# Changing the order of a convolution's inverse transforms, and the queue of attention's loads, in a two-layer diffusion trunk

## The chip, the cores and the metric

The kernel runs on one core of a Trainium2 chip. The metric is the device time of one execution in microseconds; several runs are made and their median is taken. A separate execution is profiled; its trace shows every instruction with its engine, start, duration and the tiles that it writes and reads. Five engines work beside each other: TensorE (PE, with its weight loads as PEld), VectorE (DVE), ScalarE (ACT), GpSimd (POOL) and SyncE (SP). Each takes its instructions in order. DMA transfers are issued from the instruction stream of an engine, here from SP or from POOL.

## The reference

The input is a sequence of 1024 latent tokens and 256 context tokens of width 1024. Layer 0 normalises and projects them once; half of the channels go through neighbourhood attention (8 heads of 64; each query sees a window of 8 x 16 grid places and all context keys), the other half through a bidirectional gated delta rule. Layer 1 is a Hyena layer: two long convolutions by FFT with gates between. Cut to what the change touches:

```python
def one_row(r):                     # neighbourhood attention, for each of 16 grid rows
    s_win = jnp.einsum('bqhd,brqkhd->bhqrk', qr, kw) + bias
    s_ctx = jnp.einsum('bqhd,bkhd->bhqk', qr, kc)
    p = jax.nn.softmax(jnp.concatenate([s_win.reshape(b, h, GRID_W, nwin), s_ctx], axis=-1), axis=-1)
    return p_win @ vw + p_ctx @ vc

def long_conv(u, h_fwd, h_bwd, skip):
    y_f = irfft(rfft(u, n) * rfft(h_fwd, n), n)[:length]
    y_b = irfft(rfft(u[::-1], n) * rfft(h_bwd, n), n)[:length][::-1]
    return y_f + y_b + u * skip

z = x1 * long_conv(v, filt[:, 0, 0], filt[:, 0, 1], skip[0])    # first convolution
y = x2 * long_conv(z, filt[:, 1, 0], filt[:, 1, 1], skip[1])    # second convolution
return s + gate * ((y * silu(g)) @ w_out)
```

All data are float32. Large products are made from float32r parts: a value is split into a rounded high part and the rest, the low part, and three of the four partial products are added up (`mm3`, `gemm_steps`).

## The kernel before

Everything runs on tiles of 128 partitions. A scheduler at build time gives each engine's instructions a fixed order, by priorities and a simulated time line. Two things bind it. Matrix products and transposes that go through `mm` (L116) and `tr` (L121) are pinned while `self.pinned` is set, so PE works in the order in which the program is written. And `keep_in_program_order` pins an instruction behind the one that was written just before it for the same engine; other instructions may move ahead.

**Filler.** PE's order is woven by hand. `self.fill(n)` takes n products from a generator of independent matrix products and puts them between two steps whose data need time. In attention the filler is `dn_out` (the delta heads' part of layer 0's output projection, accumulator `do`, added to `dx` in L1128 and stored by SP in L1129). In layer 1 it is `hy_stream`, the input projection.

**Attention (`natten`).** The heads are worked on in 4 pairs p; a pair has 8 column blocks j and 2 heads u, so there are 64 units in a row. A unit's scores are four products (`na_scores`): the query tile nq against the high and the low part of the keys, nkh and nkl, once for the context and once for the window. DVE adds the bias nbias and reduces (L1059), ACT takes the exponential (L1060). Two units later PE transposes the result (`na_transpose`, pt) and DVE and ACT copy it (pts, L1073); two units after that the values are multiplied (`na_values`, pv), and DVE finishes with L1094 and L1095.

`na_unit` prepares a pair and head: the bias is loaded from SP (L1016), and nq, nkh and nkl by six transfers from POOL (L1021). Each of the six fills 64 partitions, from 64 rows of the scratch arrays nq_d and nk_d that the projection stage has written: for v = 0 partitions 0 to 63, for v = 1 partitions 64 to 127. The query tile has its high part above its low part; each key tile has the same rows twice. The tiles are of type float32r, and the source is read as float32r by a bitcast. Sizes are 256 KB for nq and 320 KB for nkh and nkl. For the first pair all transfers are issued before the loop. For pair p + 1 they begin at unit 4 of pair p, two at a time, all pinned; two sets of buffers take turns.

SP issues nearly all other transfers: the raw tiles dyr (L1103) and dx (L1106) of `dn_out`, the output weights ewo_raw (L1372), the values bnv and the gate ny. `split` then makes the two parts of a raw tile: the high part on ACT (L102, for example dyh), the low part on POOL or DVE (L105). ewo_raw is first multiplied by a gate on POOL (L1384).

**Layer 1.** For each of 8 channel blocks there are two convolutions, objects of the class `Conv`: `first` on v, `second` on z. Each goes through the steps fold, transpose, dft, bins, product, idft and unfold, and the loop in `layer1` weaves the two together:

```python
second.product(); first.dft(); first.bins(); self.fill(FILL_D[2])
second.idft(); ...; y = second.unfold(); ...
first.product(); self.fill(FILL_D[3]); first.idft()
```

(FILL_D[2] is 20, FILL_D[3] is 64, and 56 products come before the next transpose.) `bins` writes the spectrum U on DVE (L1741 to L1744; the last two read the accumulator bo). `product` multiplies it with the filter's spectrum in U itself (L1753 to L1762, L1758 and L1759 being the last for the part that is used directly). Then it makes W, the high and low part of some rows of U: hWh on ACT (L1766) and hWl on DVE (L1767), each in a small piece and a large one. Last it makes Z on DVE (L1769 and L1770). `idft` then multiplies Z, one part of U, and W with the inverse matrices. It has four accumulators of 512 columns, p1, q1, pq2 and pq3 (the trace calls them p, q and pq), which come from a pool of four buffers, the same that `dft` uses for be, bo and br of the other convolution. `unfold` needs pq3 for its first step, pq2 for its second, and p1 and q1 for its third.

Of the kernel before, what the change touches and what calls it, by code (L numbers as in the profile page):

```python
# [10 lines left out]
F32 = mybir.dt.float32  # L11
F32R = mybir.dt.float32r
# [8 lines left out]
P = 128  # L21
# [40 lines left out]
class Kernel:  # L62
# [944 lines left out]
    def na_unit(self, p, u, nb):  # L1007

        nc = self.nc
        nm = f"{p}{u}"  # L1010
        rows = slice(64 * u, 64 * u + 64)
        q = nb.tile([P, L], F32R, name="nq" + nm, tag="nq")
        k = [nb.tile([P, LA], F32R, name=f"nk{n}" + nm, tag="nk" + n) for n in "hl"]
        bias = nb.tile([P, 1152], F32, name="nbias" + nm, tag="nbias")
        keep = self.tc.keep_in_program_order
        loads = [lambda: (keep if p else lambda ins: ins)(nc.sync.dma_start(bias, self.ap["na_bias"][2 * p + u]))]  # L1016
        for v in range(2):
            half = slice(64 * v, 64 * v + 64)
            for dst, src in ((q, self.nq_d[p][v]), (k[0], self.nk_d[p][0]), (k[1], self.nk_d[p][1])):
                loads.append(lambda dst=dst[half], src=src[rows, :]:  # L1020
                             keep(nc.gpsimd.dma_start(dst, src.bitcast(F32R))))  # L1021
        return (q, *k, bias), loads

    def na_pair(self, p):
# [631 lines left out]
    def idft(self, ps, Y, mat):  # L1656
        for k, y in enumerate(Y):
            self.mm(ps, y, mat[:, k, :], start=k == 0, stop=k == len(Y) - 1)

    def unfold(self, y, p, z, m):  # L1660

        nc = self.nc
        h = m // 2
        pat = {2: "p m -> p m", 3: "p (m b) -> p m b", 4: "p (m b two) -> p m b two"}[len(p.shape)]
        kw = {2: {}, 3: {"b": 2}, 4: {"b": 2, "two": 2}}[len(p.shape)]
        a, b, c = (t.rearrange(pat, **kw) for t in (y[:, 0:h], y[:, m:h:-1], z[:, 0:h]))
        nc.vector.tensor_tensor(a, p, c, ALU.add)
        nc.vector.tensor_tensor(b, c, p, ALU.subtract)
        nc.vector.tensor_copy(y[:, h:h + 1], z[:, h:h + 1])


class Conv:
# [99 lines left out]
    def idft(self):  # L1772
        k, mats, W, Z = self.k, self.mats, self.W, self.Z
        p1, q1, pq2, pq3 = self.ps = [self.psf.tile([P, 512], F32, name=n + self.nm, tag="f")
                                      for n in ("p1", "q1", "pq2", "pq3")]
        for b in range(2):
            sl = slice(b * P, b * P + P)
            k.idft(pq2[:, sl], [Z[:, 0, b, :]], mats[f"ia{b}"])
            k.idft(pq2[:, 256 + b * P:384 + b * P], [Z[:, 1, b, :]], mats[f"ib{b}"])
            k.idft(p1[:, sl], [Z[:, 0, 2 + b, :]], mats[f"ia{b}"])  # L1780
            k.idft(q1[:, 256 + b * P:384 + b * P], [Z[:, 1, 2 + b, :]], mats[f"ib{b}"])
        k.idft(pq3[:, 0:128], [self.U[:, 0, 6, :]], mats["ia0"])
        k.idft(pq3[:, 128:256], [self.U[:, 1, 6, :]], mats["ib1"])
        for ps, terms in ((pq3[:, 256:512], ((0, 2, "icc", 0), (1, 2, "iss", 0))),
                          (p1[:, 256:512], ((0, 0, "ico", 0), (0, 1, "ico", 1))),
                          (q1[:, 0:256], ((1, 0, "iso", 0), (1, 1, "iso", 1)))):
            terms = [t + ab for ab in PARTS for t in terms]
            for i, (s, j, name, n, a, b) in enumerate(terms):
                k.mm(ps, W[b][:, s, j, :], mats[name + "r"][a][:, n, :], start=i == 0, stop=i == len(terms) - 1)

    def unfold(self):
        k, nc = self.k, self.k.nc
# [164 lines left out]
```

## Time and profile before

| | us |
|---|---|
| median of 3 runs | 1907.99 |
| lowest, highest | 1900.15, 1911.63 |
| profiled execution | 1902.58 |
| its span, first to last instruction | 1900.8 |

The granted clock of PE is 0.96 of full speed over the span. In 40 slices of 47.5 us each, a digit is the busy share in tenths:

```profile
PE   6799988899998997999988899889999999999898
...
DVE  5899988756677834555566565759999989999876
...
DMA  8545455222424557454589863543433432443344
```

Attention is in slices 20 to 24 (of 0 to 39), where the DMA engines are busiest after the start. Layer 1's loop runs from about slice 27 to slice 38; there DVE is nearly as busy as PE.

In answers of the trace, a row names engine, line, operation and `out<-in` tiles, and in brackets how long the engine stood idle before it and what ended that. Times are from the start of the span. The instruction named as having ended a wait is the one that finished last by the profile; another that finished just before can be the true one.

### The profile page before, as it was taken

The page shows a single profiled execution, that of the slowest core. Times are in us where ns is not written, and L with a number is a line of the kernel's source. Part 1 is how long each engine was busy: PE and PEld are TensorE (multiplying, and loading weights), DVE is VectorE, ACT ScalarE, POOL GpSimd, SP SyncE. Part 2 cuts the span into 40 slices and gives each one's busy share as a digit, 9 for nine tenths or more (in the row PEclk, how much of TensorE's full clock was granted, in tenths as well). Part 3 has the DMA queues.
Part 4 walks back from the last instruction along what each step waited for, and adds up shares of the span by engine and source line. Part 5 has one row for each costly group of instructions (what it writes and reads, how often), then busy time and mean ns, then how long its engine had stood idle before and what let it go on. Part 6 is the DMA issues. An engine that isn't in the chain of part 4 may idle for free.

```text
span 1900.8 us, 30378 instructions
## 1 busy us (share of the span) xinstructions
PE 1734.8 (91%) x11124; PEld 1408.9 (74%) x11124; DVE 1417.5 (75%) x2847; ACT 842.6 (44%) x1830; POOL 582.4 (31%) x860
## 2 busy tenths in 40 slices
PE   6799988899998997999988899889999999999898
PEld 2366755688886775878877787778788788888686
DVE  5899988756677834555566565759999989999876
ACT  4557574444535432333344444544343434434321
POOL 0665554310193865721035401330000000000410
PEclk9889997999997998999999999999999999999999
DMA  8545455222424557454589863543433432443344
GB/s 287 167 117 158 136 187 170 107 73 103 149 94 116 163 173 229 145 131 155 158 230 230 227 192 85 185 113 93 121 108 83 105 104 72 113 128 106 108 131 139
DMA packets 162912, 270.53 MB, mean 142 GB/s; under 512 B 76953, under 2 KB 98985, under 8 KB 160714
## 3 DMA queue, kind: packets, MB, share of 16 engines
q1 hardware_dynamic: 152538, 230.83, 38.4%
q0 software_dynamic: 10224, 37.75, 10.2%
q8 instruction: 88, 1.44, 0.3%
q14 instruction: 62, 0.51, 0.1%
HBM read 192.50 MB, written 76.03 MB: 141 GB/s over the span
## 4 chain that ended last, share of the span: by engine, by line
PE 59%; DVE 21%; DMA 8%; POOL 4%; ACT 4%; issue 3%; SPq 1%; DVEq 0%; ACTq 0%; POOLq 0%
PE hx L116 6%; PE fo L116 4%; PE hg L116 3%; PE pa L116 3%; PE hu L116 2%; PE nk L116 2%; PE nv L116 2%; PE nq L116 2%; PE pq L116 2%; DVE ff L1169 2%; PE z L116 2%; PE dn L112 2%; PE dn L110 2%; PE dn L111 2%; PE pv L116 2%
## 5 line engine op out<-in xcount | busy, mean ns | idle before, releaser
L763 POOL TENSOR_TENSOR sub<-Lb,Xb 80x31 f32<-80x31 f32 (+15 forms) x124 | 87.2, 703 | 67.4 <-DMA Lb<-lsc_d 39.7
L116 PE MATMUL hx<-h1h,w1x_lo 128*128 128x512 f32 x256 | 101.0, 395 | 0.3 <-DMA w1x_lo<-in_w 0.3
L116 PE MATMUL hx<-h1l,w1x_hi 128*128 128x512 f32 x256 | 101.1, 395 | 0.0
L116 PE MATMUL hx<-h1h,w1x_hi 128*128 128x512 f32 x256 | 100.9, 394 | 0.0
L112 PE MATMUL dn<-hh,wdn_lo 128*128 128x512 f32 (+1 forms) x256 | 95.0, 372 | 0.9 <-DVE wdn_lo L105 0.9
L110 PE MATMUL dn<-hh,wdn_hi 128*128 128x512 f32 (+1 forms) x256 | 94.7, 370 | 0.0
L111 PE MATMUL dn<-hl,wdn_hi 128*128 128x512 f32 (+1 forms) x256 | 94.6, 370 | 0.0
L660 DVE SCALAR_TENSOR_TENSOR dacc<-dpad,convw,dacc 128x1024 f32<-128x1024 f32 (+1 forms) x80 | 75.9, 977 | 21.1 <-ACT dacc L658 20.2
L765 POOL TENSOR_TENSOR Xb<-Xb,sub 80x31 f32<-80x31 f32 (+15 forms) x124 | 82.9, 668 | 9.1
L1060 ACT ACTIVATE pr<-pr,st 128x640 f32<-128x640 f32 (+1 forms) x64 | 51.3, 802 | 54.1 <-DVE st L1059 54.0
L121 PE MATMUL pt<-ident,pr 128*128 128x128 f32 x304 | 46.4, 278 | 11.0 <-ACT pts L1073 6.7
L112 PEld LDWEIGHTS dn<-hh,wdn_lo 128*128 128x128 f32 x256 | 48.7, 190 | 9.8 <-DVE wdn_lo L105 1.3
L1180 ACT COPY fx<-fx_ps 128x512 f32<-128x512 f32 (+1 forms) x96 | 43.4, 484 | 27.9 <-PE fx_ps L121 24.6
L116 PEld LDWEIGHTS hx<-h1h,w1x_lo 128*128 128x128 f32 x256 | 48.1, 188 | 9.5 <-DMA w1x_lo<-in_w 0.7
L121 PE MATMUL fx_ps<-ident,ff 128*128 128x128 f32 x288 | 49.9, 299 | 5.7 <-ACT fx L1180 3.6
L1289 PE MATMUL fh<-fhh,w3s 128*128 128x512 f32 x64 | 38.2, 599 | 18.6 <-DVE fh L1291 18.6
L116 PEld LDWEIGHTS hx<-h1h,w1x_hi 128*128 128x128 f32 x256 | 48.1, 188 | 9.0
L116 PEld LDWEIGHTS hx<-h1l,w1x_hi 128*128 128x128 f32 x256 | 48.2, 188 | 8.9
L111 PEld LDWEIGHTS dn<-hl,wdn_hi 128*128 128x128 f32 x256 | 48.8, 191 | 8.0 <-issue 0.5
L110 PEld LDWEIGHTS dn<-hh,wdn_hi 128*128 128x128 f32 x256 | 48.8, 191 | 7.4
L121 PEld LDWEIGHTS pt<-ident,pr 128*128 128x128 f32 x304 | 36.3, 141 | 22.4 <-ACT pts L1073 9.3
L1313 POOL TENSOR_TENSOR fp<-fh,fh 128x1024 f32<-128x1024 f32 x16 | 39.4, 2461 | 42.4 <-ACT fh L1299 42.4
(576 smaller groups left out, 5920.1 us busy)
## 6 DMA issues: line engine op xcount, KB each, us to landing
hG<-g_d SPq DMA_DIRECT2D x16, 1088.0 KB
g_d<-G SPq DMA_DIRECT2D x16, 1024.0 KB
em_w<-in_em_w SPq DMA_DIRECT2D x24, 512.0 KB
om_w<-in_om_w SPq DMA_DIRECT2D x24, 512.0 KB
wz_raw<-in_w0z SPq DMA_DIRECT2D x16, 512.0 KB
w1x_raw<-in_w SPq DMA_DIRECT2D x16, 512.0 KB
w1x_lo<-in_w POOLq DMA_DIRECT2D x16, 512.0 KB, 7.6
wdn_raw<-in_w0dn SPq DMA_DIRECT2D x12, 512.0 KB
```

Source lines behind the costliest of these rows:

```text
L110: nc.tensor.matmul(ps, wh, xh, start=start, stop=False)
L111: nc.tensor.matmul(ps, wh, xl, start=False, stop=False)
L112: nc.tensor.matmul(ps, wl, xh, start=False, stop=stop)
L116: ins = self.nc.tensor.matmul(*args, **kw)
L121: ins = self.nc.tensor.transpose(out, x, self.ident)
L660: nc.vector.scalar_tensor_tensor(acc[:, t0:t0 + n], pad[:, o + j:o + j + n], cw[:, blk, j:j + 1], acc[:, t0:t0 + n], ALU.mult, ALU.add)
L763: nc.gpsimd.tensor_tensor(tv, Lb[:, j + 1:, j:j + 1].broadcast_to([80, m, c]), Xb[:, j:j + 1, 0:c].broadcast_to([80, m, c]), ALU.mult)
L765: nc.gpsimd.tensor_tensor(Xb[:, j + 1:, 0:c], Xb[:, j + 1:, 0:c], tv, ALU.subtract)
L1060: nc.scalar.activation(pr[:, :n], pr[:, :n], AF.Exp, bias=st[:, 0:1], scale=-1.0, accum_out=st[:, 1:2])
L1180: nc.scalar.copy(out[:, j0:j0 + m, :].rearrange("p a b -> p (a b)"), ps[:, :m * P])
L1289: nc.tensor.matmul(ps, ws[:, od, :], hh[:, sl], start=True, stop=False)
L1313: nc.gpsimd.tensor_tensor(pp[:, :L], hf[:, :L], hb[:, :L], ALU.add)
```

## The change

Two places are edited.

`na_unit`: the transfers of nq, nkh and nkl are issued from SP, except those with p = 0 and v = 0, which stay on POOL. On SP they are written as plain float32 words: the destination is read as float32 by a bitcast, the source is left as it is. They stay pinned by `keep_in_program_order`, now on SP's queue. 42 of the 48 transfers move.

`Conv.idft`: the loop over Z's eight products is moved from the beginning to the end. U's two products and the three groups of W products come first. The products themselves, their accumulators and `unfold` are the same.

```diff
@@ na_unit
             for dst, src in ((q, self.nq_d[p][v]), (k[0], self.nk_d[p][0]), (k[1], self.nk_d[p][1])):
-                loads.append(lambda dst=dst[half], src=src[rows, :]:
-                             keep(nc.gpsimd.dma_start(dst, src.bitcast(F32R))))
+
+                eng = nc.sync if p or v else nc.gpsimd
+                loads.append(lambda dst=dst[half], src=src[rows, :], eng=eng:
+                             keep(eng.dma_start(*((dst, src.bitcast(F32R)) if eng is nc.gpsimd else (dst.bitcast(F32), src)))))
@@ Conv.idft
-        for b in range(2):
-            sl = slice(b * P, b * P + P)
-            k.idft(pq2[:, sl], [Z[:, 0, b, :]], mats[f"ia{b}"])
-            k.idft(pq2[:, 256 + b * P:384 + b * P], [Z[:, 1, b, :]], mats[f"ib{b}"])
-            k.idft(p1[:, sl], [Z[:, 0, 2 + b, :]], mats[f"ia{b}"])
-            k.idft(q1[:, 256 + b * P:384 + b * P], [Z[:, 1, 2 + b, :]], mats[f"ib{b}"])
+
         k.idft(pq3[:, 0:128], [self.U[:, 0, 6, :]], mats["ia0"])
         k.idft(pq3[:, 128:256], [self.U[:, 1, 6, :]], mats["ib1"])
         for ps, terms in ((pq3[:, 256:512], ((0, 2, "icc", 0), (1, 2, "iss", 0))),
                           (p1[:, 256:512], ((0, 0, "ico", 0), (0, 1, "ico", 1))),
                           (q1[:, 0:256], ((1, 0, "iso", 0), (1, 1, "iso", 1)))):
             terms = [t + ab for ab in PARTS for t in terms]
             for i, (s, j, name, n, a, b) in enumerate(terms):
                 k.mm(ps, W[b][:, s, j, :], mats[name + "r"][a][:, n, :], start=i == 0, stop=i == len(terms) - 1)
+        for b in range(2):
+            sl = slice(b * P, b * P + P)
+            k.idft(pq2[:, sl], [Z[:, 0, b, :]], mats[f"ia{b}"])
+            ...
```

More of the change, by code (lines that the diff above doesn't have):

```diff
@@ L1789, in idft @@
                 k.mm(ps, W[b][:, s, j, :], mats[name + "r"][a][:, n, :], start=i == 0, stop=i == len(terms) - 1)
+        for b in range(2):
+            sl = slice(b * P, b * P + P)
+            k.idft(pq2[:, sl], [Z[:, 0, b, :]], mats[f"ia{b}"])
+            k.idft(pq2[:, 256 + b * P:384 + b * P], [Z[:, 1, b, :]], mats[f"ib{b}"])
+            k.idft(p1[:, sl], [Z[:, 0, 2 + b, :]], mats[f"ia{b}"])
+            k.idft(q1[:, 256 + b * P:384 + b * P], [Z[:, 1, 2 + b, :]], mats[f"ib{b}"])
     def unfold(self):
```

## The prediction

> **What bounds the kernel now.** I read the page first: engine shares, then the chain of waits that ended last.
>
> ```profile
> span 1900.8 us, 30378 instructions
> ## 1 busy us (share of the span) xinstructions
> PE 1734.8 (91%) x11124; PEld 1408.9 (74%) x11124; DVE 1417.5 (75%) x2847; ACT 842.6 (44%) x1830; POOL 582.4 (31%) x860
> ...
> PE 59%; DVE 21%; DMA 8%; POOL 4%; ACT 4%; issue 3%; SPq 1%; DVEq 0%; ACTq 0%; POOLq 0%
> ```
>
> TensorE (PE) is busy 91% of the span, so an edit pays only where it shortens one of PE's waits or the half-clock stretch that follows a long one. VectorE (DVE) comes second. The change touches two stages, so next comes the table by stage: attention (950 to 1180 us), and two turns of the second layer's loop over channel blocks, an early one and a late one. Columns: length, then the busy time of PE, PEld, DVE, ACT and POOL, PE's clock, the DMA share and GB/s.
>
> ```profile
> 950.00:1180.00 230.00, 207.01 (x1696) 174.04 (x1695) 148.59 (x408) 107.46 (x285) 69.92 (x83) 0.98 0.76 195
> ...
> 1356.00:1423.00 67.00, 63.16 (x360) 54.72 (x360) 60.41 (x96) 25.22 (x40) 4.12 (x23) 0.97 0.39 101
> ...
> 1690.00:1757.00 67.00, 66.29 (x385) 57.62 (x384) 62.13 (x97) 28.47 (x45) 5.15 (x24) 1.00 0.40 106
> ```
>
> In attention PE leaves 23 us idle and the DMA engines are busy 76% of the time. In the loop PE is full late (66.3 of 67), while early both PE (63.2) and DVE (60.4) lack some: there they wait for each other. The view of waits says for what; first attention, then the loop (total, times, longest):
>
> ```profile
> PE pt L121 <- ACT pts L1073: 6.7, 4, 4.4
> ...
> PE do L116 <- DVE dx L1128: 2.5, 2, 2.2
> ...
> PE s L116 <- DMA nkl<-nk_d: 0.9, 1, 0.9
> ...
> PE s L116 <- DMA nkh<-nk_d: 0.2, 1, 0.2
> ```
>
> ```profile
> PE pq L116 <- DVE hZ L1769: 12.6, 4, 4.3
> ...
> PE pq L116 <- ACT hWh L1766: 2.7, 4, 0.7
> ...
> PE pq L116 <- DVE hU L1744: 0.4, 1, 0.4
> ```
>
> So PE waits 15.3 us in front of the inverse transforms. That and some 8 us of attention is all that the two edits can reach directly.
>
> **Edit 1, the loads.** There are 16 each of nq, nkh and nkl; 6 of the first pair stay on POOL and 42 go to SP.
>
> ```profile
> L1021 POOL DMA_DIRECT2D nq<-nq_d x16: 512/552/582, 961.4 to 1088.2; - x16
> ...
> DMA to landing us min/median/max: 3.7/11.8/17.3
> ```
>
> ```profile
> L1059 DVE CUSTOM_DVE_ANT_0 pr<-s,nbias x56: 670/816/825, 985.7 to 1166.8; 128x640 f32<-128x640 f32 x48, 128x512 f32<-128x512 f32 x8
> L1016 SPq DMA_DIRECT2D nbias<-in_na_bias x8: 382/427/774, 954.8 to 1098.7; - x8
> ```
>
> The first two rows are the loads on POOL, the last two the scores' reduction (64 units from 985.7 to 1166.8, so 2.8 us each) and the price of an issue on SP. POOL is freed of 42 x 0.55 = 23 us, but with 70 us of work in 230 it bounds nothing. SP's queue gains 42 x 0.43 = 18 us of issuing. Each moved load is pinned behind the previous SP transfer of the program, so it can queue behind a store of dx that waits for DVE; behind the loads queue the raw loads of dyr, dx and the output weights, in SP's order. The buffers of the next pair are free by then, so the loads themselves hold nobody long, and they start in units 4 to 10 of a pair for use in unit 16. Six units are 17 us of cover. If it is gone, a pair starts late by a landing time, 3.7 to 17.3 us in the old queue.
>
> What the loads do to other transfers matters more. Here are two stretches, one with POOL's loads alone (15 us, 965 to 980) and one with SP's transfers alone (10 us, 985 to 995); columns are packets, MB, share of 16 engines:
>
> ```profile
> q0 software_dynamic: 797, 3.07, 112.4%
> ```
>
> ```profile
> q1 hardware_dynamic: 1559, 3.14, 85.7%
> ```
>
> POOL's queue fills the engines at 3.07 MB / 15 us = 205 GB/s, SP's moves 314 GB/s at 86%. The moved bytes are 42 x 0.3 = 12.5 MB: 61 us of full engines before, 40 us after. Where that hurts shows at 1047 us, where ScalarE (ACT) stands in front of a cast whose input was requested 23 us before, beside POOL's loads, and the scores queued behind it stand too:
>
> ```profile
> 1027.44 0.38 SPq L1103 DMA_DIRECT2D dyr<-y_d  x1
> ```
>
> ```profile
> 1050.49 0.62 ACT L102 CAST dyh<-dyr 128x512 fp32r<-128x512 f32 x1 [3.74 <-DMA dyr<-y_d]
> ```
>
> ```profile
> 1052.24 1.23 PE L121 MATMUL pt<-ident,pr 128*128 128x128 f32 x5 [4.43 <-ACT pts L1073]
> ```
>
> ```profile
> 1052.40:1055.80 3.40, 3.40 (x13) 3.11 (x13) 2.63 (x8) 2.09 (x5) 2.37 (x4) 0.50 1.01 400
> 1359.60:1363.00 3.40, 3.40 (x19) 3.40 (x18) 0.95 (x4) 0.37 (x1) 0.17 (x3) 0.50 0.17 35
> 1424.50:1427.80 3.30, 3.17 (x15) 3.20 (x16) 3.30 (x5) 0.68 (x2) 0.00 (x0) 0.50 0.93 223
> ```
>
> PE loses 4.4 us, then runs 3.4 us at half clock, which costs 1.7 more. With the 0.9 + 0.2 us for nkl and nkh, the loads cost 7.2 us that I can point at. Bounds: a gain of 11 if the 2.5 us for dx and more go too; a loss of 6, if a cast on ACT is again queued before data that are late. I take a gain of 7: what is late next is the softmax chain, whose single waits here are below 2 us.
>
> The Trainium skill, DMA: Bandwidth & Descriptors, under queues, rings and completion order, says that each DMA engine takes turns between queues by packets and keeps order within one ring. By that rule dyr lost its protection: it now stands behind every load ahead of it. The trace disagrees on the worth of that protection, since dyr took 23 us with a queue to itself; by the rule alone edit 1 would gain nothing, and that is the second rival below.
>
> **Edit 2, the order of the inverse transform.** A late second transform, as it is:
>
> ```profile
> 1600.94 0.68 DVE L1769 TENSOR_TENSOR hZ<-hU 128x512 f32<-128x512 f32 x1
> ...
> 1601.77 0.46 PE L116 MATMUL pq<-dft_ia,hZ 128*128 128x128 f32 x2 [0.71 <-ACT hWh L1766]
> ...
> 1602.74 0.67 DVE L1744 TENSOR_TENSOR hU<-hU,bo 128x512 f32<-128x512 f32 x1
> ...
> 1603.34 0.68 DVE L1767 TENSOR_TENSOR hWl<-hU,hWh 128x512 fp32r<-128x512 f32 x1
> ...
> 1603.63 0.39 PE L116 MATMUL pq<-dft_ia,hU 128*128 128x128 f32 x2
> ...
> 1604.78 0.39 PE L116 MATMUL p<-dfth_ico,hWh 128*128 128x256 f32 x2
> ...
> 1605.25 0.40 PE L116 MATMUL p<-dfth_ico,hWl 128*128 128x256 f32 x2
> ...
> 1605.96 0.40 PE L116 MATMUL q<-dfth_ico,hWl 128*128 128x256 f32 x2
> ```
>
> Z's first half is ready at 1601.62 and PE starts 0.15 later. Z's products take 1603.63 - 1601.77 = 1.86; U's and the first W group 1.15; the next products until hWl is wanted 0.47; from there to the end (1606.36) 1.11; 4.59 in all. The point is hWl: DVE writes it **after** Z and after two operations of the other convolution, ready at 1604.02. New order, with PE free at 1601.77 - 0.71 = 1601.06: 1.15 + 0.47 bring it to 1602.68, it waits for hWl until 1604.15, then 1.11 + 1.86 end it at 1607.1. That is 0.7 us **later**. Z was not what came last; the split of W was. Four second transforms have that 0.7 us wait today: +2.8. The other three wait for nothing at the start: there hWl can add between 0 and 0.7, and the one with the wait for L1744 can lose those 0.4; I take +0.2 for the three, together +3.
>
> A first transform with a long wait:
>
> ```profile
> 1354.01 1.22 DVE L1758 TENSOR_TENSOR hU<-hU,ht 128x1024 f32<-128x1024 f32 x1
> ...
> 1356.95 0.42 DVE L1767 TENSOR_TENSOR hWl<-hU,hWh 128x256 fp32r<-128x256 f32 x1
> ...
> 1358.00 0.62 ACT L1766 CAST hWh<-hU 128x512 fp32r<-128x512 f32 x1 [2.33 <-DVE hU L1762]
> ...
> 1358.71 0.46 PE L116 MATMUL pq<-dft_ia,hZ 128*128 128x128 f32 x2 [3.79 <-DVE hZ L1769]
> ...
> 1359.09 0.68 DVE L1767 TENSOR_TENSOR hWl<-hU,hWh 128x512 fp32r<-128x512 f32 x1
> ```
>
> PE is free at 1354.92. In the new order U starts at 1355.4 (after L1758), W's first group waits for the small hWl (1357.5), the next for hWh (1358.7), then for the large hWl (1359.9), and 1.11 + 1.86 end it at 1362.9. Before: 1358.71 + 4.59 = 1363.3, plus 1.7 for the half-clock stretch from 1359.6 (row above) = 1365.0. The gain is 2.1 if the clock stays up, 0.4 if not; PE is still idle for most of the 3.4 us before 1359.6, so I take 1 for this wait and the 4.3 us one, 0.5 for the other two: 3 us in all. Five others wait for nothing: 0.
>
> The Trainium skill, TensorE: Matmul & The Clock Gate, in its part on the HAM clock gate, says that the clock halves after an idle window of some 3.4 us. By that rule three split waits would keep it up, and the three slow stretches of the loop would save 3 x 1.7 = 5 us. The trace is stricter: it shows half clock (1424.5) after a wait of only 1.9 us.
>
> Last, what follows on DVE: the unfolding takes pq3 first and needs pq2 last, since Z's products now end everything. Before, it worked on pq2 while W ran. About 1 us of DVE work moves behind PE's end in each transform; PE's 56 or 64 fill products cover it, except in the three or four turns where DVE leads: between 0 and +4, I take +2. Edit 2: +3 - 3 + 2 = **+2 us**.
>
> **Sum.** -7 + 2 = -5 us. The profiled execution took 1902.6 us (its span and 1.8 us around it), so 1897.6; the median of the runs, 1908.0, is 5.4 above it, so on that scale **1903**.
>
> **Rivals.**
> - *Both waits shrink* (0.16). The schedule puts the split of W ahead, the clock stays up, and attention loses the dx waits too: -11 in attention, -5 in the loop, about 1892. For it: one small DVE operation there took 3.1 us while POOL, behind its loads, caught up:
> ```profile
> 1014.16 3.10 DVE L1094 TENSOR_TENSOR nr<-nr,ny 128x128 f32<-128x128 f32 x1 [1.20 <-ACT nr L1093]
> ```
>   Against: DVE's order follows from hWh's cast, which is not changed.
> - *The loads only change queues* (0.20): dyr waits behind them in one ring, ACT stands as before; edit 2 leaves +2: 1910. Against: 314 against 205 GB/s. It covers that the pinned loads are issued late.
> - *The output buffer* (0.12), slower. pq3 is written first now. It waited for L1744, the last release of the four buffers; if it keeps that buffer, a second transform can start only at 1602.74 + 0.67 + 0.1 = 1603.5 and ends 4.59 later, at 1608.1: +1.7, seven times 12, and about as much again where DVE leads. With edit 1's -7: +5 to +17, about 1919. It decides as soon as L1744 ends after PE is free. Against: if buffers go by first use, pq3 gets the first one free.
>
> **Numbers.** Forecast 0.47, rivals 0.16, 0.20, 0.12, and 0.05 for a schedule that shifts elsewhere. A change of 1% is 19 us, about what a measurement of this kernel tells from none: below 1889 lies half of the first rival and a little of the forecast, 0.12; above 1927 a third of the third rival and the rest's worse half, 0.07. The range, 1886 to 1919, reaches from the first rival's middle to the third's.
>
> **What would show it.** Right: POOL's queue nearly empty in attention, dyr landing within 10 us, no ACT wait of 3 us before dyh, no half clock at 1052; in the loop PE's waits move from hZ to hWl. Wrong: waits for L1744 at the first product (third rival), or hWl written before hZ (first).

## The result and the profile after

The changed kernel takes 1934.8 us (median of 6 runs, 1931.5 to 1942.8), the kernel before 1908.2 us on the same chip. The ratio is 1.0155, with a 95% interval of 1.013 to 1.018: 1.3% to 1.8% slower, some 27 us. The forecast was 1903 us, with a range that ended at 1919.

The page of the changed kernel, the lines that answer to those shown of the kernel before:

```profile
span 1933.5 us, 30376 instructions
## 1 busy us (share of the span) xinstructions
PE 1752.7 (91%) x11124; PEld 1422.5 (74%) x11124; DVE 1417.2 (73%) x2847; ACT 838.9 (43%) x1830; POOL 563.0 (29%) x818
...
DVE 19%; PE 14%; issue 2%; ACT 2%; DMA 2%; POOL 0%; DVEq 0%; ACTq 0%; POOLq 0%; SPq 0%
...
L1669 DVE TENSOR_TENSOR hy<-p,hq 128x512 f32<-128x512 f32 x16 | 11.1, 692 | 59.5 <-POOL hq L1801 34.1
```

PE's share is still 91%, but its busy time grew by 17.9 us for the same 11124 products. The chain of waits is no help this time: its shares add up to about 40%, so much of it was not followed back. The last line was not among the costliest groups of before: VectorE (DVE) stands still for 59.5 us in front of this operation, the first of `unfold` in the new schedule, 34.1 of them because of the memsets of hq on POOL.

To see where the time is lost I take one stretch in every kernel, here called **the loop**: from the first product of the first inverse transform to the first product of the sixteenth and last. Its length is that of each kernel's one profiled execution. The view by windows gives for it the length, and then the busy time of PE, PEld, DVE, ACT and POOL, PE's clock, the DMA share and GB/s. Before:

```profile
1292.66:1811.89 519.23, 495.08 (x2818) 426.96 (x2817) 473.93 (x726) 209.46 (x331) 53.87 (x180) 0.98 0.39 103
```

After:

```profile
1290.94:1844.31 553.37, 509.69 (x2818) 436.45 (x2817) 472.83 (x726) 206.78 (x331) 53.96 (x180) 0.96 0.37 97
```

The loop is 34.1 us longer, so it holds the whole loss and a little more. PE is busy for 509.7 us instead of 495.1 with the same 2818 products, 14.6 us more, at a lower clock (0.96 instead of 0.98). By the trace's records of the clock, PE is busy at half clock for 38.5 us of this loop instead of 15.5, which makes (38.5 - 15.5) / 2 = 11.5 of the 14.6 us; the other 3.1 are left unexplained. The other 19.5 us of the loop are new idle time of PE (43.7 instead of 24.2). DVE's work is the same to about 1 us (473 and 474).

Who waits for whom in the loop is in the view of waits, from 1290 to 1860 us (total us, times, longest). Before:

```profile
POOL hq L1798 <- PE q L116: 86.3, 13, 16.3
...
ACT hq L1801 <- PE q L116: 26.9, 11, 3.7
...
PE hx_ps L121 <- DVE hf L1169: 0.3, 1, 0.3
```

After:

```profile
POOL hq L1801 <- PE q L116: 133.3, 15, 19.4
...
ACT hq L1802 <- PE q L116: 70.6, 13, 6.4
...
DVE hy L1669 <- POOL hq L1801: 34.1, 8, 5.9
...
PE hx_ps L121 <- DVE hf L1171: 12.9, 7, 3.4
...
PE pq L116 <- DVE hU L1760: 9.2, 4, 2.7
...
PE p L116 <- DVE hWl L1769: 5.6, 5, 1.4
PE pq L116 <- DVE hWl L1769: 5.3, 5, 1.5
```

PE's part of this adds up to the new idle time: 12.6 us more for the transposes' input hf, 8.8 more for U (0.4 before) and 10.9 for hWl, less the 12.6 us for Z that are gone, make 19.7.

The first line of before was there to be read ahead of the prediction, and I did not read it: 13 times the memset of hq waits for a product of q, though a memset needs no product. What it waits for is the **buffer**. `unfold` takes its tile hq with the tag "hZ", which has one buffer, the one in which Z lies. So hq may be written only when the last product that reads Z is done. Before, Z's products came first and the buffer was free 2.0 us into the transform shown below; now Z's products are the last of it, and everything in `unfold` queues behind them. One late second transform after the change shows it, from its first product to the end of `unfold` (start, duration, engine, operation, and in brackets the idle time ahead and its end):

```profile
1693.65 0.38 PE L116 MATMUL pq<-dft_ia,hU 128*128 128x128 f32 x2
...
1696.11 0.68 DVE L1769 TENSOR_TENSOR hWl<-hU,hWh 128x512 fp32r<-128x512 f32 x1
...
1696.84 0.50 PE L116 MATMUL p<-dfth_ico,hWl 128*128 128x256 f32 x2 [1.40 <-DVE hWl L1769]
...
1699.45 0.39 PE L116 MATMUL q<-dft_ib,hZ 128*128 128x128 f32 x2
...
1699.92 0.59 ACT L1802 COPY hq<-q 128x512 f32<-128x512 f32 x1 [5.48 <-PE q L116]
...
1699.95 0.16 POOL L1801 MEMSET hq<- 128x1 f32 x3 [8.64 <-PE q L116]
...
1700.61 0.69 DVE L1669 TENSOR_TENSOR hy<-p,hq 128x512 f32<-128x512 f32 x1 [3.83 <-ACT hq L1802]
...
1705.29 1.22 DVE L1820 TENSOR_TENSOR hy<-hy,hyt 128x1024 f32<-128x1024 f32 x1
```

And the kernel before, the transform that the prediction shows from 1601.77 to 1606.36:

```profile
1603.40 0.39 PE L116 MATMUL q<-dft_ib,hZ 128*128 128x128 f32 x2
...
1603.90 0.17 POOL L1798 MEMSET hq<- 128x1 f32 x3 [5.36 <-PE q L116]
...
1604.35 0.43 DVE L1667 TENSOR_TENSOR hyd<-pq,hq 128x256 f32<-128x256 f32 x1 [0.33 <-ACT hq L1801]
...
1609.53 1.23 DVE L1817 TENSOR_TENSOR hy<-hy,hyt 128x1024 f32<-128x1024 f32 x1
```

Before, Z is read until 1603.79, the memset follows 0.11 us later, and DVE unfolds from 1604.35 on, 2 us ahead of the last product's end at 1606.36. `unfold` ends at 1610.76, **4.40 us** after that product. After, the last product ends at 1699.84, it is one of Z's, memset and copies follow it, and `unfold` ends at 1706.51, **6.67 us** after. The same difference stands in nearly every transform: over all 16 these tails add up to 73.9 us before and to 110.1 us after.

### The profile page after: what moved, and what is told of

Same layout as the page of the kernel before. It is cut to its first block, busy times and chain, and to the rows that moved or that the text cites. A ratio compares the mean times of both kernels' runs of the same rounds, so it can differ in the third digit from the quotient of the medians.

```text
span 1933.5 us, 30376 instructions
## 1 busy us (share of the span) xinstructions
PE 1752.7 (91%) x11124; PEld 1422.5 (74%) x11124; DVE 1417.2 (73%) x2847; ACT 838.9 (43%) x1830; POOL 563.0 (29%) x818
## 5 line engine op out<-in xcount | busy, mean ns | idle before, releaser
L121 PE MATMUL hx_ps<-ident,hf 128*128 128x128 f32 x256 | 42.1, 292 | 16.4 <-DVE hf L1171 15.6
L1669 DVE TENSOR_TENSOR hy<-p,hq 128x512 f32<-128x512 f32 x16 | 11.1, 692 | 59.5 <-POOL hq L1801 34.1
L121 PEld LDWEIGHTS hx_ps<-ident,hf 128*128 128x128 f32 x256 | 33.7, 151 | 27.5 <-DVE hf L1171 19.0
```

The costliest lines, as they stand in the source:

```text
L121: ins = self.nc.tensor.transpose(out, x, self.ident)
```

## The experiments

Ratios are to the kernel before on the same chip, with their 95% interval. "Loop" is the stretch defined above, "tail" the time from a transform's last product to the end of `unfold`.

The theories: A, hq must wait for Z's buffer. B, beside A: even with a free buffer `unfold` ends late, because its inputs are completed late. C: PE must wait for W's low part (hWl), which DVE writes after Z. R: the moved loads do the harm.

### One edit at a time

The moved loads alone, that is the kernel before with

```diff
-                loads.append(lambda dst=dst[half], src=src[rows, :]:
-                             keep(nc.gpsimd.dma_start(dst, src.bitcast(F32R))))
+                eng = nc.sync if p or v else nc.gpsimd
+                loads.append(lambda dst=dst[half], src=src[rows, :], eng=eng:
+                             keep(eng.dma_start(*((dst, src.bitcast(F32R)) if eng is nc.gpsimd else (dst.bitcast(F32), src)))))
```

> The kernel before with the moved loads alone. If the loss of 26.6 us comes from the order of the inverse transform (theories A, B, C), attention keeps the gain that the traces show, about 4 us, and the loop stands as before: 1904 us (1900 to 1909). If the loads do the harm (theory R: a queue shifts later work), it is above 1915.

Measured: 1903.6 us, ratio 0.9977 (0.9953 to 1.0001).

```profile
1292.34:1812.86 520.52, 496.12 (x2818) 427.97 (x2817) 474.70 (x726) 209.31 (x331) 53.96 (x180) 0.98 0.39 103
```

The loop is the one of before to 1.3 us. The new order alone, that is the kernel before with

```diff
-        for b in range(2):
-            sl = slice(b * P, b * P + P)
-            k.idft(pq2[:, sl], [Z[:, 0, b, :]], mats[f"ia{b}"])
...
                 k.mm(ps, W[b][:, s, j, :], mats[name + "r"][a][:, n, :], start=i == 0, stop=i == len(terms) - 1)
+        for b in range(2):
+            sl = slice(b * P, b * P + P)
+            k.idft(pq2[:, sl], [Z[:, 0, b, :]], mats[f"ia{b}"])
...
```

> The kernel before with the new order of products alone. A, B and C: the loop loses what it lost in the changed kernel, without the 4 us that attention gave: 1938 us (1932 to 1945), the milestones 4 to 8 us later per turn. R: below 1920.

Measured: 1939.9 us, ratio 1.0161 (1.0124 to 1.0198), and a loop of 553.1 us, as in the changed kernel (553.4). So the whole loss is in the order of the products, and theory R, that the loads do harm, falls.

### The buffer, and the low split of W

A, B and C are left. First hq in another buffer, that of hx; the last transform keeps the old one, because there the other is used for output rows:

```diff
-        qz = self.tile([P, 900], "hq", "hZ")
+        qz = self.tile([P, 900], "hq", "hZ" if self.o and self.cb == KT - 1 else "hx")
```

> The changed kernel, with the unfolding's reversed copies (hq) in the buffer of hx instead of that of Z; nothing else is edited. Theory A (all of the loss is that hq must wait until Z's last product has read Z): the time from the last product to the end of unfold falls from 6.67 us to the 4.40 of before, and the kernel to about 1908. Theory B (the order alone: z2 needs pq2 and z1 needs q1, and both are now completed by Z's products at the very end, so only the part of unfold that reads pq3 can move ahead): 5.4 us instead of 6.67, 16 times 1.3 = 20 us, about half of it covered by PE's filling: 1924 (1918 to 1930). Theory C (PE's waits for W's low part): 1935, unchanged.

Measured: 1911.5 us, ratio 1.0012 (0.9985 to 1.0038).

```profile
1291.02:1819.98 528.96, 502.90 (x2818) 433.52 (x2817) 472.06 (x726) 209.44 (x331) 53.75 (x177) 0.97 0.38 101
```

The median tail falls from 6.67 to 4.53 us, all but 0.13 of the way to the 4.40 of before, and the loop gives 24.4 of its 34.1 us back. The waits for the transposes' input and for U, 12.9 and 9.2 us in the changed kernel, all but go with it:

```profile
PE hx_ps L121 <- DVE hf L1171: 0.7, 2, 0.5
PE pq L116 <- DVE hU L1760: 0.4, 1, 0.4
```

So these two were DVE's lateness behind `unfold`. Theory A has most of the loss. B's 5.4 us did not come: I had added up the copies on ScalarE (ACT) and the operations on DVE, and they run side by side. pq2 is complete 0.45 us ahead of the end, and while DVE works on it, ACT copies q.

Second, the changed kernel without the wait for the low part: each product that should read W's low half reads the high half instead, so W's correction term is not computed, and DVE still writes the low half.

```diff
-                k.mm(ps, W[b][:, s, j, :], mats[name + "r"][a][:, n, :], start=i == 0, stop=i == len(terms) - 1)
+                k.mm(ps, W[0][:, s, j, :], mats[name + "r"][a][:, n, :], start=i == 0, stop=i == len(terms) - 1)
```

> The changed kernel with W's high part read in place of its low part: as many products of the same shape, W's correction term is not computed and nothing on PE waits for the low split, which DVE still writes. Theory C: the transforms shrink from 6.4 us on average (101.7 us for 16) to about 4.9, 16 times 1.46 = 23 us, less what filling covers: 1915 (1910 to 1922). Theories A and B: unfold still begins after the last product and takes 6.67 us from there; a transform that ends earlier lets DVE start earlier only where the transform waited, so 1927 to 1935.

Measured: 1922.1 us, ratio 1.0080 (1.0046 to 1.0113).

```profile
1289.40:1833.45 544.05, 507.01 (x2818) 437.19 (x2817) 472.62 (x726) 206.98 (x331) 53.85 (x180) 0.96 0.38 99
```

The ratio falls from 1.0155 to 1.0080, some 14 us of the time, and the loop by 9.3 us: between what C and what A and B expected. The tails stay (109.8 us for the 16). So C is the second cause, and the smaller one. Do the two add up? Both edits in one kernel, with the same part left out:

> The changed kernel with both edits of the last two runs: hq in the buffer of hx, and W's high part read in place of its low part (its correction term is not computed). If the buffer (23 us back, 1934.8 to 1911.5) and the waits for the low split (12.7 us back, to 1922.1) are two costs one behind the other, they add up: 1899 (1894 to 1904), below the kernel before, since U's products then start ahead of Z for nothing. If both hide the same stretch, little is left to gain beside the first: 1908 to 1912.

Measured: 1894.2 us, ratio 0.9926 (0.9897 to 0.9956).

```profile
1293.47:1804.88 511.41, 493.85 (x2819) 427.08 (x2817) 471.92 (x726) 209.23 (x331) 53.64 (x177) 0.98 0.40 105
```

In the time they add up (2.3% of the time of before, against 1.4% + 0.8%), in the loop to more: 42 us, against 24.4 + 9.3 = 33.7 one by one. This loop is 7.8 us **shorter** than before, in a kernel that leaves out W's correction. So there is something in the new order: U's and W's products do start while DVE still works on Z. With the loops of these four kernels the change can be taken apart: 519.2 before; 511.4 with the new order if nothing waits for the low split or the buffer; 529.0 with the waits for the low split (+17.6); 553.4 with the shared buffer as well (+24.4).

### The buffer by itself

In the runs so far U and W had moved too. Here only two of each transform's products move, p's and q's of Z's last element, in the kernel before:

```diff
             k.idft(pq2[:, sl], [Z[:, 0, b, :]], mats[f"ia{b}"])
             k.idft(pq2[:, 256 + b * P:384 + b * P], [Z[:, 1, b, :]], mats[f"ib{b}"])
-            k.idft(p1[:, sl], [Z[:, 0, 2 + b, :]], mats[f"ia{b}"])
-            k.idft(q1[:, 256 + b * P:384 + b * P], [Z[:, 1, 2 + b, :]], mats[f"ib{b}"])
+            if b == 0:
+                k.idft(p1[:, sl], [Z[:, 0, 2 + b, :]], mats[f"ia{b}"])
+                k.idft(q1[:, 256 + b * P:384 + b * P], [Z[:, 1, 2 + b, :]], mats[f"ib{b}"])
...
                 k.mm(ps, W[b][:, s, j, :], mats[name + "r"][a][:, n, :], start=i == 0, stop=i == len(terms) - 1)
+        k.idft(p1[:, P:2 * P], [Z[:, 0, 3, :]], mats["ia1"])
+        k.idft(q1[:, 384:512], [Z[:, 1, 3, :]], mats["ib1"])
```

> The kernel before, with two of each transform's products (p and q of Z's last element) moved behind W's, everything else in its place: U, W and their waits as before, Z's last read 4.5 us after the transform's begin instead of about 1.9. Theory A: unfold waits for it in full, 6.7 us from the last product to its end instead of 4.4, and the loop grows by most of the 24 us that mending the buffer gave back: 519 us to 538 (534 to 544), the kernel to 1927 (1922 to 1933). If the shared buffer costs only together with the late low split, less than 8 us: 1912.

Measured: 1945.0 us, ratio 1.0214 (1.0174 to 1.0254): at least what the whole change costs.

```profile
1298.42:1854.84 556.42, 509.06 (x2819) 436.72 (x2818) 472.59 (x726) 206.78 (x331) 53.69 (x180) 0.96 0.37 96
```

Three of its waits, from 1290 to 1860 us (total us, times, longest):

```profile
DVE hy L1667 <- POOL hq L1801: 36.2, 8, 6.9
...
PE pq L116 <- DVE hZ L1769: 22.5, 5, 7.1
...
PE hx_ps L121 <- DVE hf L1169: 12.9, 7, 3.4
```

The loop grows by 37.2 us, and the tails by 36.2 (to 110.1, as in the changed kernel). The waits show the way: DVE waits for hq as it does after the change; because it then ends `unfold` and `fold` late, PE waits for the transposes' input (hf) as after the change, and now also longer for Z, 22.5 us instead of 12.6. The expectation had the way right and half of the size (19 us of the loop): I had taken the 24 us of the run above, where the early start of U's products had paid for a part.

The same two products at the end, with hq in the buffer of hx:

> The same with hq in the buffer of hx. Theory A: nothing is left of the loss, 4.4 to 4.5 us from the last product and a loop of 519 to 521 us: 1908 (1904 to 1911). If it is the late completion of p and q that holds the unfolding, it stays near the run without the buffer's mending.

Measured: 1902.4 us, ratio 0.9993 (0.9972 to 1.0013).

```profile
1291.54:1808.03 516.49, 494.98 (x2818) 425.60 (x2817) 473.96 (x726) 209.35 (x331) 53.87 (x177) 0.99 0.40 104
```

Nothing is left of the loss: 42.6 us come from the choice of the buffer in the line that takes the tile. The tails are 77.6 us, 3.7 more than before, and cost nothing that shows. So what held `unfold` was, but for these 3.7 of 36.2 us, not that p and q were late but that Z's buffer was. The control is the same edit in the kernel before, where Z is read first:

> The kernel before with hq in the buffer of hx and nothing else. With Z's products first, the shared buffer is free 2.1 us into the transform and holds nobody: 4.40 us from the last product to the end of unfold in both, and 1908 (1904 to 1911), no difference. If hq's wait there (86 us of POOL's idle time is put down to it) cost time already, up to 16 x 0.5 us less: 1900.

Measured: 1907.7 us, ratio 1.0008 (0.9989 to 1.0028), with a loop of 519.2 us, the length of before. There the shared buffer costs nothing that can be measured.

### Can the new order be made to pay?

Order U, Z, W, the order in which DVE delivers, with hq in the buffer of hx (in the changed kernel W's products and the loop over Z change places):

```diff
         k.idft(pq3[:, 128:256], [self.U[:, 1, 6, :]], mats["ib1"])
+        for b in range(2):
+            sl = slice(b * P, b * P + P)
...
         for ps, terms in ((pq3[:, 256:512], ((0, 2, "icc", 0), (1, 2, "iss", 0))),
...
-        for b in range(2):
-            sl = slice(b * P, b * P + P)
...
```

> The changed kernel with hq in the buffer of hx and the products in the order U, Z, W: only W's products come after Z's. If what hurt is the buffer and the low split's lateness, neither is left: transforms of 4.6 us, 4.4 us from the last product to the end of unfold, and 1903 (1898 to 1908), as with the loads alone. If starting with U's products hurts by itself (the accumulator pq3 taking a buffer late), transforms get longer and it stays above 1910.

Measured: 1903.4 us, ratio 0.9988 (0.9966 to 1.0009), loop 520.8 us. Starting with U's products does no harm and brings nothing by itself. Next, the low split earlier. In `product` the difference that W needs is written first, into a buffer that is free, so that ACT's cast runs beside the sum that Z needs:

```diff
-        v.tensor_tensor(U[:, :, 8:10, :], U[:, :, 0:2, :], U[:, :, 2:4, :], ALU.add)
-        v.tensor_tensor(U[:, :, 2:4, :], U[:, :, 0:2, :], U[:, :, 2:4, :], ALU.subtract)
+        D = t0[:, 0:4].rearrange("p (s a) b -> p s a b", s=2)
+        v.tensor_tensor(D, U[:, :, 0:2, :], U[:, :, 2:4, :], ALU.subtract)
+        v.tensor_tensor(U[:, :, 8:10, :], U[:, :, 0:2, :], U[:, :, 2:4, :], ALU.add)
...
-        for dst, src in ((slice(2, 3), slice(7, 8)), (slice(0, 2), slice(2, 4))):
-            nc.scalar.copy(W[0][:, :, dst, :], U[:, :, src, :])
-            v.tensor_tensor(W[1][:, :, dst, :], U[:, :, src, :], W[0][:, :, dst, :].bitcast(F32), ALU.subtract)
+        for dst, src in ((slice(2, 3), U[:, :, 7:8, :]), (slice(0, 2), D)):
+            nc.scalar.copy(W[0][:, :, dst, :], src)
+            v.tensor_tensor(W[1][:, :, dst, :], src, W[0][:, :, dst, :].bitcast(F32), ALU.subtract)
```

With the new order U, W, Z and hq in the buffer of hx:

> The changed kernel with hq in the buffer of hx, and in the product U's difference written first, into ht0, so that ScalarE's cast of W's high part runs beside U's sum: in DVE's program W's large low split then stands ahead of three operations of the other convolution (3 x 0.67 us) in the second transforms, and behind Z as before in the first. Everything is computed. If what is left of the loss is that PE waits for the low split (1911.5 with the buffer mended, 1894.2 with the waits cut out by reading the high part), about half to two thirds of these 17 us come back: second transforms of 4.6 us instead of 6.1, and 1902 (1897 to 1907). If the waits are only where other DVE work shows, 1911.

Measured: 1900.0 us, ratio 0.9963 (0.9943 to 0.9984), below both kernels by its interval.

```profile
1285.23:1805.83 520.60, 500.66 (x2819) 431.32 (x2817) 473.15 (x726) 209.38 (x332) 53.85 (x177) 0.98 0.39 103
```

Compared with the same kernel without the earlier split (1911.5 us, loop 529.0) the loop is 8.4 us shorter. So the lateness of the low split was a real cost and could be mended by the order of two operations on DVE. It was mended in the second transforms alone, where PE's waits for hWl fall from 5.6 us in all to 0.5; in the first ones they grow from 5.3 to 8.2. But the loop is no shorter than before's; that this kernel is 0.4% faster than the one before must come from somewhere else. Its profile arrives at the loop at 1285.2 us, the one of before at 1292.7, and that of the next run, whose code ahead of the loop is the same, at 1295.5. Where the 0.4% come from is left open.

The same with the order U, Z, W:

> The same two edits of buffer and product, with the order U, Z, W, which is the order in which DVE delivers. No wait for the low split inside a transform, 4.53 us for each second one: 1898 (1893 to 1903), below both kernels. If DVE's own chain sets the turns whatever the order, 1903, as with order U, Z, W without the earlier split (1903.4).

Measured: 1906.5 us, ratio 0.9998 (0.9980 to 1.0015), loop 520.9 us. And the kernel before with the moved loads and the earlier split, order Z, U, W:

> The kernel before with the moved loads and the product's difference first; the order Z, U, W stays, and hq in Z's buffer. There Z is what comes last before the transform (12.6 us of PE's waits in four first transforms), and the earlier split takes away only the 0.7 us waits for W's high part in four second ones: 1902 (1898 to 1906), 0 to 3 us below the loads alone.

Measured: 1906.9 us, ratio 1.0002 (0.9982 to 1.0023), loop 522.2 us. In both the expected gain did not come. Eight kernels with four orders of the products, the kernel before among them, have loops of 516 to 522 us, once hq is free in time and no low split is far behind. Where the order hardly matters, something else sets the length; DVE's chain, busy 473 to 475 us in them, is the likely one, but this was only argued.

Last, less work for DVE: two multiplications of a turn given to POOL (here in the kernel with the moved loads).

```diff
-                nc.vector.tensor_tensor(gt, gt, self.hy["x2", cb][:, :L], ALU.mult)
+                nc.gpsimd.tensor_tensor(gt, gt, self.hy["x2", cb][:, :L], ALU.mult)
...
-                nc.vector.tensor_tensor(y, y, self.hy["g", cb], ALU.mult)
+                nc.gpsimd.tensor_tensor(y, y, self.hy["g", cb], ALU.mult)
```

> The kernel before with the moved loads, and two multiplications of the second layer (the gate by x2, and y by the gate, 128x1024 each) given from DVE to POOL, where such an operation took 2.46 us in another stage. If DVE's chain is what PE waits for in the early turns (60.4 us of 67 busy), taking 2.4 us per turn off it saves that much in four turns, and half-clock stretches with it: 1904 - 10 - 3 = 1891 (1886 to 1898). If only the order of DVE's work counts and not its amount, 1904.

Measured: 1913.5 us, ratio 1.0046 (1.0026 to 1.0065).

```profile
1283.31:1813.41 530.10, 496.35 (x2818) 426.19 (x2817) 484.74 (x710) 209.37 (x331) 104.81 (x195) 0.98 0.38 101
```

The loop is 9.6 us longer than with the moved loads alone (520.5). The two operations on POOL, by groups (busy time and mean ns of one):

```profile
L1634 POOL TENSOR_TENSOR hg<-hg,hu 128x1024 f32<-128x1024 f32 x8 | 30.6, 3831 | 4.3 <-DVE hg L1633 4.3
L1534 POOL TENSOR_TENSOR hy<-hy,hg 128x1024 f32<-128x1024 f32 x7 | 21.4, 3053 | 17.4 <-DVE hy L1819 17.4
```

They took 3.8 and 3.1 us there, not the 2.46 of the other stage. And DVE did not get less to do: it has 16 operations fewer in the loop (710 against 726) and is busy 484.7 us, 10.0 **more** than with the moved loads alone (474.7). Operations that run beside POOL's got longer, as L1763 here (shortest, median and longest ns), first in this kernel, then with the moved loads alone:

```profile
L1763 DVE TENSOR_TENSOR hU<-hU x16: 677/684/2774, 1279.2 to 1806.3; 128x512 f32<-128x512 f32 x16
```

```profile
L1763 DVE TENSOR_TENSOR hU<-hU x16: 681/687/694, 1288.3 to 1807.6; 128x512 f32<-128x512 f32 x16
```

Three of these 16 stand beside an operation of POOL, and each takes 2.77 us instead of 0.68; in the same way five multiplications of U take 3.4 us instead of 1.2 (L1755 and L1756). The 33 operations of DVE that overlap with POOL's 15 take 58.4 us; with the median times that the same kinds have elsewhere in this loop they would take 31.2. The planner also put other work where the two had been on DVE: two operations on hu (2.6 us) now run ahead of `unfold` in late first transforms, which have tails of 6.2 us instead of 4.5. With the order U, Z, W:

> Order U, Z, W, hq in the buffer of hx, the moved loads, and the two multiplications on POOL: the two gains together, if there are two. 1890 (1884 to 1897) if DVE's load bounds the early turns, 1903 if not.

Measured: 1916.3 us, ratio 1.0047 (1.0027 to 1.0068), loop 535.4 us, with DVE busy 485.4 us of it. Both expectations missed, and neither run tests whether less work for DVE is a gain, since DVE was busy for longer in both. That the loop grew about as much as DVE's busy time (9.6 and 10.0 us in the first) fits a loop set by DVE, but does not show it.

## Why the prediction was wrong

**Edit 2, the term "+2" for what follows on DVE.** This is the step that failed. The prediction said that "About 1 us of DVE work moves behind PE's end in each transform" and that "PE's 56 or 64 fill products cover it", except in three or four turns. What moved is 2.27 us in each of 16 transforms, 36 us in all, since not the reading of pq2 but the buffer that hq shares with Z decides when `unfold` may begin. And it is not covered: PE's waits for the transposes' input grew from 0.3 to 12.9 us, seven times up to 3.4 us, and those for U from 0.4 to 9.2. Shown by three runs: taking hq out of the buffer gave 24.4 us of the loop back, and reading Z late, with all else in its place, cost 37 us and with hq elsewhere nothing. I followed the products and their accumulators and did not ask which buffers the moved reads release. The waits of before had the answer in their first lines.

**Edit 2, "+3 - 3" for the waits inside the transform.** The kernel to compare is the changed one with hq in the buffer of hx: its loop is 9.8 us longer than before (529.0 against 519.2), where the prediction had nothing. As idle time the sum is not far off. The way was right: waits moved from Z to hWl, 1.40 us in the late second transform shown, close to the 1.5 us that the prediction worked out for another (1604.15 - 1602.68). In the second transforms PE's waits grew from 3.1 to 5.6 us, close to the +3. In the first ones they fell only from 12.6 to 11.9 us, not by 3: PE now waits for hWh and hWl in pieces. Idle time makes 1.9 of the 9.8 us; the rest is PE's longer busy time (502.9 us against 495.1), of which the lower clock explains some 5.6 us (26.7 us busy at half clock instead of 15.5). Waiting for the low split is the part that hurts: a kernel that does not wait for it has a loop 17.6 us shorter, and 7.8 us shorter than before, but it leaves out W's correction.

**The clock.** The prediction set a rule of the Trainium skill (TensorE: Matmul & The Clock Gate, the part on the HAM clock gate: half speed after an idle window of some 3.4 us) against a wait of 1.9 us that was enough. By that rule split waits would have kept the clock up. The change split them, and the loop ran at half clock for 44.4 us instead of 17.1. What decides is told in the last section.

**Edit 1, "-7".** Measured are 2.5 us (an interval from no gain to 0.5%). That is nearer to the second rival, in which the loads only change queues. Two steps failed. First, I took the stalls of one execution for what the loads cost. In four other profiles with the loads unmoved the 4.4 us stall at 1052 us is absent, and PE waits 5.3 to 6.1 us for nkh instead of 0.2, as here, in the kernel with the new order alone:

```profile
PE s L116 <- DMA nkh<-nk_d: 6.0, 1, 6.0
...
PE pt L121 <- ACT pts L1073: 1.5, 2, 0.7
```

The changed kernel:

```profile
PE s L116 <- DMA nkh<-nk_d: 3.6, 1, 3.6
...
PE pt L121 <- ACT pts L1075: 1.2, 2, 1.0
```

So one wait or the other is there, and the move shortens the sum: from the first of the scores' products to the first of the output projection it takes 191.4 to 193.1 us in five profiles with the loads on POOL (192.1 on average) and 186.5 to 193.2 in eleven with them on SP (189.0). Second, the rates. I compared 205 GB/s of POOL's loads with 314 of SP's other transfers and gave the difference to the queue. The loads alone on SP, in 5 us of the changed kernel (1015 to 1020 us; packets, MB, share of 16 engines):

```profile
q1 hardware_dynamic: 277, 1.07, 102.7%
```

That is 1.07 MB / 5 us = 214 GB/s with the engines full, as on POOL. The rate belongs to these transfers, not to the queue. From 1012 to 1014 us of the same trace, when most packets on SP's queue (114 of 201, by their 4608 bytes) are those of the bias load, which fills 128 partitions, it moves 0.78 MB in 2 us, 390 GB/s, with the engines as full (102.5%). The Trainium skill, DMA: Bandwidth & Descriptors, under "Issuing engines are not separate DMA queues", has it that transfers share the same engines whoever starts them; the two rates here agree. And SBUF — State Buffer, under the DMA port swizzle, has it that a transfer into 64 partitions, as these are, reaches half of the ports, about 218 GB/s of 436. The 205 and 214 agree, and so does the faster bias load; no run here changed the shape of the loads alone, so that this is the reason is not shown.

**The rivals.** The output buffer (pq3 in the buffer freed last, 1919) was on the right side and fell: its sign, a wait for L1744 (L1746 after the change) in front of the first product, is not among the waits of after. It was the right kind of question, asked of the wrong buffer. "Both waits shrink" fell with the waits for hWl. None of the rivals let anything behind PE's last product become longer by more than a few us; I had priced the new order by PE's own waits.

## What to carry to other kernels

When reads are moved, list for each buffer they release who takes it next, and read the profile's waits for an instruction that waits for something it has no data from: a memset waiting for a product is a shared buffer showing itself. A buffer shared in time costs nothing as long as its last reader is early, and an order of products can depend on that without a word in the code. A stall seen in one execution is a term of a sum only if other executions show it too. And when work is given to another engine, the durations of what stays have to be looked at, not only their number.

## What the runs showed of the hardware

The granted clock goes by a fixed grid of 3.41 us, and what decides is not a wait but the idle time within one step of the grid. In all sixteen profiles, between 1290 and 1822 us, PE was at full clock in 2364 steps. After 72 of them the next step was at half clock: PE had been idle for 1.61 to 3.41 us of them. After the other 2292 the clock stayed up: idle 1.89 us at most. Only a few steps lie in the overlap, so about half of a step, 1.7 us, is the border here, in however many pieces. Two steps of the changed kernel with their successors (columns as for the loop):

```profile
1430.07:1433.48 3.41, 1.27 (x6) 0.73 (x4) 3.41 (x4) 3.41 (x4) 0.81 (x3) 1.00 0.27 43
1433.48:1436.89 3.41, 2.83 (x10) 2.28 (x10) 3.41 (x5) 0.47 (x2) 0.18 (x1) 0.50 0.99 352
1648.51:1651.92 3.41, 1.92 (x17) 1.72 (x16) 3.41 (x6) 0.32 (x1) 0.00 (x0) 1.00 0.97 265
1651.92:1655.33 3.41, 3.41 (x28) 3.28 (x28) 0.74 (x1) 0.62 (x2) 0.30 (x5) 1.00 0.57 115
```

2.14 us idle, and the next step is at 0.50; 1.49 us idle, and it stays at 1.00. The Trainium skill (TensorE: Matmul & The Clock Gate, the part on the HAM clock gate) has the free-running window of 3.4 us, and these traces agree; its idle window need not be idle throughout, though. This is why the new waits cost more than their length: with 19.5 us more of idle time came 27.3 us more at half clock, which cost some 11.5 us.

DVE and POOL are not independent either. Beside an operation of POOL with two inputs, an operation of DVE with two inputs took up to 3.42 us instead of 1.22, or 2.77 instead of 0.68, in the two kernels with multiplications on POOL. Why is not shown here.
